# Columns of six weight units stored in another order and read back in the natural one by TensorE's access pattern

## The chip, the cores and the metric

The kernel runs on one core of one Trainium2 chip, in one launch. The metric is the device time of that launch in microseconds; the number given for a kernel is the median of its runs. The profile is one more execution, taken by the hardware profiler, with its own time.

The engines are named as in the profile: PE is TensorE (matmuls), PEld its weight loads, DVE is VectorE, ACT is ScalarE, POOL is GpSimd, SP issues most DMAs. A matmul has a stationary operand, which is loaded ahead as weights, and a moving operand, which is streamed through; its result is added up in PSUM.

## The reference: what is computed

One layer of a bidirectional encoder for 256 tokens of width 2,048. Twelve windowed attention heads and four Fourier groups make 2,048 features per token; they are normalised in two parts and go through the output projection, which the change touches. Then comes a feed-forward block with a convolution.

```python
        a = _rmsnorm(_window_attention(q, k, v, sink), attn_out_g)
        f = _rmsnorm(_fourier_mix(u, w_fourier), fourier_out_g)
        x = x + jnp.concatenate([a, f], axis=-1) @ w_out
        x = x + _conv_ffn(_rmsnorm(x, norm2_g), w_up, dw_w, dw_b, w_down)
    return _rmsnorm(x, normf_g)
```

`w_out` is 2,048 x 2,048 in float32.

## The kernel before

All large products are made in split float32: each operand is written as a high part (rounded to the type fp32r, which PE streams) and a low part, and three matmuls, high by high, low by high and high by low, are added in PSUM.

The weights come in *units* of 128 partitions x 2,048 values (1 MB). `load` (L166) issues a unit's DMA on SP into one of three `raw` buffers; `split` makes the high part with a Copy on ScalarE (L174) and the low part with a subtraction on VectorE (L175), both into a `parts` buffer (again three). `unit(i, work)` runs the matmuls of unit i and then splits unit i + 2 and loads further ones, so that splitting is two units ahead of PE and loading more. The order of the work on each engine is that of the program text; the small steps of attention and of the norms are hung before, beside or behind certain units (`at`, `run`).

The output projection has 16 units (`OUT_ORDER`, in the loop at L807). A unit is a pair (c, kq): the 512 output columns of block c, and the four k tiles (128 rows of `w_out` each) of group kq. The host lays them out with `moving` in `_layout`: for k tile q of the unit, `wout[n, :, 512 * q : 512 * (q + 1)]` holds its 128 rows in the partitions and its 512 columns side by side. In the output projection the weights are thus the *moving* operand, and the stationary one is a 128 x 128 piece of the activations, `cat` (the high part, then the low part of a tile, made by `feature_out`).

`moving_weights` (L339) makes the matmuls of a unit for one block of 128 tokens, b: for each k tile q, L345 streams the high weights against the high activations, L346 the high weights against the low activations, and L347 the low weights against the high activations. With two blocks and four k tiles that makes 24 matmuls of 512 columns in a unit, and 384 in the projection. Their results go to the PSUM tiles `ps_a` (groups 0 to 2, the attention features) and `ps_ff` (group 3, the Fourier features). The moving operand is one run of 512 adjacent values in each partition:

```python
            wh, wl = hi[:, q * n : (q + 1) * n], lo[:, q * n : (q + 1) * n]
```

When a group is complete, `out_add` (L766) adds the scaled sums to the residual `xs` on VectorE; when both groups of a block c are in, its columns are transposed on PE (`turn_x_in`, L789) for the next stage. The other callers of `moving_weights` are the projection of the values (`ps_v`, L602) and a part of the down projection (`ps_l`, L1199).

## Time and profile before

| | us |
|---|---|
| median of 3 runs | 946.41 (946.23 to 946.63) |
| the profiled execution | 945.75 |
| its span, first to last instruction | 944.0 |
| the first and last start of the output projection's matmuls | 162.1 and 256.5 |

The page of the profile gives the busy time of each engine, the chain of waits that ended last, and groups of equal instructions with busy time, mean duration, and the idle time of the engine just before them with what ended it. The timeline gives instructions in the order of time (start, duration, engine, line, operation, tiles, shape). A matmul's duration reaches from the start of its stream to its last result, and overlaps with the next matmul; the distance between two starts is what a matmul takes from PE. The granted clock of TensorE was 0.998 in the mean over the span.

### The profile page before, as it was taken

To read this page: it belongs to the slowest core of one execution; us is meant where nothing else is said; L and a number is where in the kernel's file an instruction comes from. 1 tells how busy PE (TensorE), PEld (TensorE's weight loads), DVE (VectorE), ACT (ScalarE), POOL (GpSimd) and SP (SyncE) were. 2 spreads that over 40 slices of the span, in tenths; PEclk is the share of its full clock that TensorE was granted. 3 is DMA by queue.
4 is the path that set the end of the run, shared out by engine and by line. 5 is a ranking of instruction groups with operands and counts; after the bars stand their busy time and mean duration, and the time that the engine had idled before them with its cause. 6 is when DMAs were issued, how large, how long until landed. Compare 5 with 4: busy or idle time off the path is not lost.

```text
span 944.0 us, 15017 instructions
## 1 busy us (share of the span) xinstructions
PE 934.7 (99%) x6275; PEld 857.6 (91%) x6275; DVE 711.1 (75%) x817; ACT 536.6 (57%) x624; POOL 48.2 (5%) x64
## 2 busy tenths in 40 slices
PE   9999999999999999999999999999999999999996
PEld 8889998888888999999999999999999999999985
DVE  7568877666667766869776887768878678889695
ACT  7656766554454645446555565555555555655544
POOL 0000000000000000000000000000000000000003
PEclk9999999999999999999999999999999999999999
DMA  9864544456558677677798778787787978779742
GB/s 361 312 224 137 176 140 173 134 179 202 195 223 271 220 232 238 188 241 238 250 261 257 243 238 274 249 264 228 261 242 238 298 249 256 248 217 265 222 176 89
DMA packets 32628, 215.00 MB, mean 228 GB/s; under 512 B 3600, under 2 KB 3856, under 8 KB 8240
## 3 DMA queue, kind: packets, MB, share of 16 engines
q1 hardware_dynamic: 28448, 184.55, 53.7%
q0 software_dynamic: 4112, 29.49, 16.5%
q8 instruction: 49, 0.80, 0.3%
q14 instruction: 19, 0.16, 0.0%
HBM read 211.93 MB, written 2.10 MB: 227 GB/s over the span
## 4 chain that ended last, share of the span: by engine, by line
PE 99%; POOL 0%; ACT 0%; issue 0%; DVE 0%; ACTq 0%; POOLq 0%
PE ps_val L375 22%; PE ps_gate L375 21%; PE ps_q L362 5%; PE ps_P L1081 3%; PE ps_P L1080 3%; PE ps_P L1079 3%; PE ps_N L1080 3%; PE ps_N L1081 3%; PE ps_N L1079 3%; PE ps_q L364 2%; PE ps_u L257 2%; PE ps_a L347 2%; PE ps_a L345 2%; PE ps_a L346 2%; PE ps_gate L362 2%; PE ps_val L362 2%
## 5 line engine op out<-in xcount | busy, mean ns | idle before, releaser
L175 DVE TENSOR_TENSOR parts<-raw,parts 128x2048 fp32r<-128x2048 f32 (+1 forms) x129 | 293.5, 2275 | 72.9 <-ACT parts L174 72.8
L174 ACT ACTIVATE parts<-raw 128x2048 fp32r<-128x2048 f32 (+1 forms) x129 | 245.9, 1906 | 82.2 <-PE ps_gate L375 19.9
L375 PEld LDWEIGHTS ps_val<-hU,parts 128*128 128x128 f32 x1824 | 211.6, 188 | 2.2
L375 PE MATMUL ps_val<-hU,parts 128*128 128x256 f32 x1824 | 212.9, 276 | 0.0
L375 PEld LDWEIGHTS ps_gate<-hU,parts 128*128 128x128 f32 x1776 | 206.4, 188 | 2.5
L375 PE MATMUL ps_gate<-hU,parts 128*128 128x256 f32 x1776 | 207.3, 276 | 0.0
L362 PE MATMUL ps_q<-hT,parts 128*128 128x512 f32 x192 | 66.0, 395 | 0.0
L856 ACT ACTIVATE fa_v<-ps_val 128x256 f32<-128x256 f32 x38 | 14.6, 384 | 88.3 <-PE ps_val L375 88.2
L966 DVE TENSOR_TENSOR parts_N<-sumw,parts_N 128x2048 fp32r<-128x2048 f32 x18 | 41.2, 2291 | 21.2 <-ACT parts_N L965 21.1
L1079 PE MATMUL ps_P<-parts_P,op_P 128*128 128x512 f32 x144 | 56.0, 389 | 0.0
L1080 PE MATMUL ps_P<-parts_P,op_P 128*128 128x512 f32 x144 | 56.0, 389 | 0.0
L1081 PE MATMUL ps_P<-parts_P,op_P 128*128 128x512 f32 x144 | 56.0, 389 | 0.0
L364 PE MATMUL ps_q<-hT,parts 128*128 128x256 f32 x192 | 51.6, 279 | 0.0
L362 PEld LDWEIGHTS ps_q<-hT,parts 128*128 128x128 f32 x192 | 35.9, 188 | 7.4
L965 ACT ACTIVATE parts_N<-sumw 128x2048 fp32r<-128x2048 f32 x18 | 34.4, 1914 | 14.3 <-PE ps_gate L375 10.6
L1079 PE MATMUL ps_N<-parts_N,op_N 128*128 128x512 f32 x108 | 42.0, 389 | 0.0
L1080 PE MATMUL ps_N<-parts_N,op_N 128*128 128x512 f32 x108 | 42.0, 389 | 0.0
L1081 PE MATMUL ps_N<-parts_N,op_N 128*128 128x512 f32 x108 | 42.0, 389 | 0.0
L345 PE MATMUL ps_a<-parts,cat 128*128 128x512 f32 x96 | 37.9, 395 | 0.0
L347 PE MATMUL ps_a<-parts,cat 128*128 128x512 f32 x96 | 37.5, 391 | 0.0
L346 PE MATMUL ps_a<-parts,cat 128*128 128x512 f32 x96 | 37.3, 389 | 0.0
L364 PEld LDWEIGHTS ps_q<-hT,parts 128*128 128x128 f32 x192 | 35.4, 188 | 0.3
(350 smaller groups left out, 1513.1 us busy)
## 6 DMA issues: line engine op xcount, KB each, us to landing
raw<-in_w_up SPq DMA_DIRECT2D x86, 1024.0 KB, 5.6
raw<-in_w_in SPq DMA_DIRECT2D x20, 1024.0 KB, 6.4
sumw<-in_w_down POOLq DMA_DIRECT2D x18, 1024.0 KB, 8.5
raw<-in_w_out SPq DMA_DIRECT2D x16, 1024.0 KB, 4.8
raw<-in_w_down_late SPq DMA_DIRECT2D x4, 1024.0 KB, 6.2
u_raw<-in_u_in SPq DMA_DIRECT2D x5, 768.0 KB, 10.8
raw<-in_w_down_last SPq DMA_DIRECT2D x4, 768.0 KB, 4.4
xs<-in_x SPq DMA_DIRECT2D x4, 512.0 KB, 15.3
```

Source lines behind the costliest of these rows:

```text
L174: nc.scalar.activation(hi, raw, AF.Copy)
L175: nc.vector.tensor_tensor(lo, raw, f32(hi), ALU.subtract)
L345: nc.tensor.matmul(ps, ah, wh, start=first and q == q0, stop=False)
L346: nc.tensor.matmul(ps, al, wh, start=False, stop=False)
L347: nc.tensor.matmul(ps, ah, wl, start=False, stop=last and q == q0 + len(kk) - 1)
L362: nc.tensor.matmul(ps, hi[:, s], h, start=k == 0, stop=False)
L364: nc.tensor.matmul(ps[:, 0:S], lo[:, s], h[:, 0:S], start=False, stop=k == NK - 1)
L375: nc.tensor.matmul(ps[:, 0:S], w[:, s], h[:, o : o + S], start=k == 0 and n == 0, stop=k == NK - 1 and n == 2,)
L966: nc.vector.tensor_tensor(lo, src, f32(hi), ALU.subtract)
L1079: nc.tensor.matmul(ps, o[:, 0, p, :], hi[:, s], start=first and p == 0, stop=False)
L1080: nc.tensor.matmul(ps, o[:, 1, p, :], hi[:, s], start=False, stop=False)
L1081: nc.tensor.matmul(ps, o[:, 0, p, :], lo[:, s], start=False, stop=end)
```

## The change

Six of the 16 units get a list of *forms*, one per k tile: units 1, 2, 4 and 6 one form for all four tiles, units 9 and 13 two forms each, for their second and fourth tile. A form (a, e, c) with a * e * c = 512 says that the host stores the 512 columns of that k tile in another order: column number ((e' * a) + a') * c + c' in the natural order stands at place ((a' * e) + e') * c + c'. `moving_weights` then describes the moving operand by three dimensions, e of step c, a of step e * c and c of step 1, so that PE reads the columns in the natural order again. The output columns in PSUM, the number and size of the DMAs, the splits and the number and order of the matmuls are as before.

In a partition, PE so reads c adjacent values, then c values that lie e * c values further, and so on for a pieces, and then begins again c values behind the first. With c = 1 there are no adjacent pairs: form (256, 2, 1) reads each second value, first the even places and then the odd ones; form (2, 256, 1) reads one value from the first half of the 512, one from the second half, and so on.

```diff
--- before.py
+++ after.py
@@ -53,6 +53,9 @@
 
 OUT_ORDER = [(0, 0), (1, 0), (0, 1), (1, 1), (0, 3), (0, 2), (1, 3), (1, 2)]
 OUT_ORDER += [(c, k) for c in (2, 3) for k in range(4)]
+
+OUT_FORMS = {1: [(2, 16, 16)] * 4, 2: [(2, 8, 32)] * 4, 4: [(4, 8, 16)] * 4, 6: [(2, 32, 8)] * 4}
+OUT_FORMS.update({9: [None, (2, 64, 4), None, (256, 2, 1)], 13: [None, (2, 256, 1), None, (8, 2, 32)]})
 
 
 GROUPS = [list(range(4))] + [list(range(k, k + 8)) for k in range(4, 36, 8)]
@@ -336,12 +339,17 @@
         nc.vector.tensor_copy(dst, spread_sums(spread_diagonals(r, name), name)[:, :S])
 
 
-    def moving_weights(hi, lo, n, kk, act, b, ps, first, last, q0=0):
+    def moving_weights(hi, lo, n, kk, act, b, ps, first, last, q0=0, forms=None):
 
         for q, k in enumerate(kk, q0):
             ah = act(k)[:, b * P : (b + 1) * P]
             al = act(k)[:, S + b * P : S + (b + 1) * P]
             wh, wl = hi[:, q * n : (q + 1) * n], lo[:, q * n : (q + 1) * n]
+            if forms and forms[q]:
+                a, e, c = forms[q]
+                wh, wl = (
+                    w.rearrange("p (a e c) -> p e a c", a=a, e=e, c=c) for w in (wh, wl)
+                )
             nc.tensor.matmul(ps, ah, wh, start=first and q == q0, stop=False)
             nc.tensor.matmul(ps, al, wh, start=False, stop=False)
             nc.tensor.matmul(
@@ -816,7 +824,7 @@
             for b in range(2):
                 moving_weights(
                     hi, lo, 512, range(4 * kq, 4 * kq + 4), cat.get, b, ps[b],
-                    kq in (0, 3), kq in (2, 3),
+                    kq in (0, 3), kq in (2, 3), forms=OUT_FORMS.get(n),
                 )
 
         unit(i, work)
@@ -1288,6 +1296,12 @@
     wout = np.concatenate(
         [moving(w_out, slice(c * 512, (c + 1) * 512))[k : k + 1] for c, k in OUT_ORDER]
     )
+    for n, forms in OUT_FORMS.items():
+        for q, form in enumerate(forms):
+            if form:
+                a, e, c = form
+                cols = wout[n, :, 512 * q : 512 * (q + 1)]
+                cols[:] = cols.reshape(P, e, a, c).transpose(0, 2, 1, 3).reshape(P, 512).copy()
     w_up = np.asarray(inp["w_up"])
     wup = np.concatenate(
         [still(w_up, o + j * P) for j in range(NF) for o in (0, DFF)]
```

## The prediction

> **What bounds the kernel now.** I read four views. First the page: busy time by engine, and the chain of waits that ended last.

> ```profile
> span 944.0 us, 15017 instructions
> PE 934.7 (99%) x6275; PEld 857.6 (91%) x6275; DVE 711.1 (75%) x817; ACT 536.6 (57%) x624; POOL 48.2 (5%) x64
> ...
> PE 99%; POOL 0%; ACT 0%; issue 0%; DVE 0%; ACTq 0%; POOLq 0%
> ```

> TensorE (PE) is busy for 99% of the span, and 99% of the chain is PE itself; issue and the other engines have 0%. A microsecond added to PE is therefore a microsecond added to the time, unless PE waits somewhere for something that comes no later. Next the costliest groups of the page, to see whether it waits in the stage that is changed:

> ```profile
> L175 DVE TENSOR_TENSOR parts<-raw,parts 128x2048 fp32r<-128x2048 f32 (+1 forms) x129 | 293.5, 2275 | 72.9 <-ACT parts L174 72.8
> L174 ACT ACTIVATE parts<-raw 128x2048 fp32r<-128x2048 f32 (+1 forms) x129 | 245.9, 1906 | 82.2 <-PE ps_gate L375 19.9
> ...
> L375 PE MATMUL ps_gate<-hU,parts 128*128 128x256 f32 x1776 | 207.3, 276 | 0.0
> ...
> L345 PE MATMUL ps_a<-parts,cat 128*128 128x512 f32 x96 | 37.9, 395 | 0.0
> L347 PE MATMUL ps_a<-parts,cat 128*128 128x512 f32 x96 | 37.5, 391 | 0.0
> L346 PE MATMUL ps_a<-parts,cat 128*128 128x512 f32 x96 | 37.3, 389 | 0.0
> ```

> The last column is idle time before the instruction: 0.0 for the three matmul lines of the output projection. The splitting Copies of ScalarE (L174) do have idle time, and what ends it is PE. So in this kernel PE sets the pace and the feeders wait.

> The mean of 389 ns is the latency of one matmul, which overlaps the next one; it is not what a matmul costs. That is the distance from start to start, so the third view is the timeline of PE, here one whole unit (12 matmuls for each of two row blocks) and, far behind it, a row of 256-column matmuls:

> ```profile
> 193.64 0.39 PE L345 MATMUL ps_a<-parts,cat 128*128 128x512 f32 x1
> 193.87 0.39 PE L346 MATMUL ps_a<-parts,cat 128*128 128x512 f32 x1
> 194.09 0.39 PE L347 MATMUL ps_a<-parts,cat 128*128 128x512 f32 x1
> ...
> 199.09 0.50 PE L485 MATMUL ps_tota<-ones,sq_a 128*128 128x1 f32 x4
> ```

> ```profile
> 500.27 3.00 PE L375 MATMUL ps_gate<-hU,parts 128*128 128x256 f32 x25
> ```

> From 193.64 to 199.09 there are 24 matmuls: 5.45 us / 24 = 227 ns each. The 25 matmuls of 256 columns take 3.00 us, of which the last one's latency is 0.276 us (L375 above): 2.72 / 24 = 113.5 ns. Twice the columns cost twice the time, so nothing fixed per matmul is left in the sum: PE takes one column of the moving operand each 227 / 512 = 0.443 ns. I call this a slot. PE reads the moving operand back to back and has no slack in which a slower read could hide.

> **The change part by part.** Nothing is added or removed on any queue: the same matmuls, splits and DMAs stand in the same order, and the DMAs carry the same bytes.

> *The permuted weights in HBM, their DMAs and the splits.* The permutation is made on the host, a row of a unit is still 2,048 contiguous values, and L174 and L175 go over it without looking at the order. Cost: 0. If a load were late, PE would show it; it has no idle time here.

> ```profile
> raw<-in_w_out SPq DMA_DIRECT2D x16, 1024.0 KB, 4.8
> ```

> *The longer description in the instruction.* The moving operand has three free dimensions in place of one. If PE's sequencer needs more time for it, this lies behind the matmul that streams: the row of 256-column matmuls shows that a weight load and a matmul are issued in 113.5 ns at the most, so 227 - 113 = 114 ns per matmul are cover. Cost: 0. Without the cover, it would be up to that much times 120 matmuls, which no row suggests.

> *The reads themselves.* This is the only term. A unit has 24 matmuls: four k tiles, two row blocks, three matmuls for each, and all three read the k tile's columns as moving operand. Units 1, 2, 4 and 6 permute all four k tiles (96 matmuls), units 9 and 13 two of four (12 each). That makes 120 matmuls, sorted by what a read looks like in a partition:
> - runs of 32, 16 or 8 adjacent values (units 1, 2, 4, 6 and the tile with form (8, 2, 32)): 102 matmuls;
> - runs of 4 adjacent values (form (2, 64, 4)): 6 matmuls;
> - no run at all, each value 8 bytes behind the last (form (256, 2, 1)): 6 matmuls;
> - no run, and each value 1,024 bytes from the last, to and fro (form (2, 256, 1)): 6 matmuls.

> No matmul of the trace reads its moving operand with steps, so the price is bounded from both sides. From below: 0, if any address is as good as the next. A gain is left out: 256-column and 512-column rows, in different stages and from different tiles, all run at the same 0.443 ns, and no row streams faster. From above, the rows where PE takes longest over a column:

> ```profile
> 0.99 4.37 PE L213 MATMUL ps_warm<-ones 128*128 128x128 f32 x20 [0.99 <-POOL ones L205]
> ...
> 205.03 1.04 PE L789 MATMUL ps_x<-ident,xs 128*128 128x128 f32 x8
> ...
> L789 PE MATMUL ps_x<-ident,xs 128*128 128x128 f32 x24 | 3.1, 273 | 0.0
> ```

> The transposes of the same stage: (1.04 - 0.27) / 7 = 110 ns for 128 columns, 0.86 ns a column, or two slots. The warm-up: ten matmuls (two records each) in 4.37 us, 3.4 ns a column, or 7.7 slots. Neither is a stepped read; they show at what rates PE can be held.

> My value: a run of 4 or more costs nothing, and a single value costs a second slot, as a column of the transposes does. The reason is the row above: the read streams 4 bytes per slot with no fixed part, so it must take neighbours together to keep up, and where the neighbour is not wanted, half of what is taken is thrown away. That gives 12 matmuls x 512 columns x 0.443 ns = 2.7 us. Bounds of this term: 0, and at the warm-up's 3.4 ns a column 12 x 512 x 2.97 = 18 us.

> *Where the added time goes.* The units lie in this stretch of PE's timeline (first and last start of a line's matmuls):

> ```profile
> L345 PE MATMUL ps_a<-parts,cat x96: 388/389/478, 162.1 to 250.6; 128*128 128x512 f32 x96
> L345 PE MATMUL ps_ff<-parts,cat x32: 389/389/476, 188.2 to 256.1; 128*128 128x512 f32 x32
> ```

> A later end of unit 9 or 13 delays the next unit's matmuls by as much; the splits for it (1.9 us on ScalarE, 2.3 us on VectorE by L174 and L175, against 5.45 us of PE per unit) only come earlier relative to PE. Nothing takes the time back later, since PE has no wait to shorten.

> Sum: the profiled execution took 945.75 us (span 944.0, and 1.75 around it); with 2.7 it would take 948.5. It lies 0.66 us under the median of 946.41 of the three runs, and the forecast is for the median: 946.41 + 2.72 = **949.1 us**.

> **The rivals.** A difference of 0.2%, 1.9 us, is about what a measurement of this kernel can tell from no change.

> *Only the to-and-fro form is slow, so the time does not move by more than that.* If what is fetched together is wide enough to hold two values that are 8 bytes apart, the form (256, 2, 1) finds two values per fetch and keeps its rate; only (2, 256, 1) changes place with each value. Place: the first of unit 13's two permuted k tiles. Price: 6 x 227 ns = 1.36 us, 947.8 us. It decides from the point at which an 8-byte step is free. For it: every other row of the trace is consistent with any width of fetch. Against it: the stream already runs at one value per slot, and nothing shows room for twice the bytes.
> [...]

> *Every break in a run costs.* If PE reads ahead along adjacent addresses and loses slots whenever the next value is elsewhere, all six units pay. Runs per matmul: 32, 16, 32 and 64 in units 1, 2, 4, 6 (24 matmuls each: 3,456), 128 for runs of 4, 512 to and fro, 16 for runs of 32 (6 matmuls each: 3,936); 7,392 breaks without the 8-byte form. At one slot: 3.3 us, 949.7. At the warm-up's extra 2.97 ns: 22 us, 968. I take two slots, near the transposes, since they run in this very stage: 6.6 us, 953.0. For it: a row after a change of work starts unevenly (the matmul at 199.45 is followed by the next only at 199.77), so PE does have a start-up in its reads. Against it: the matmuls of a row each start at a new address and pay nothing for that.

> ```profile
> 199.45 0.48 PE L345 MATMUL ps_ff<-parts,cat 128*128 128x512 f32 x1
> 199.77 0.39 PE L346 MATMUL ps_ff<-parts,cat 128*128 128x512 f32 x1
> ```

> *Any pattern with more than one free dimension leaves the fast read.* All 120 matmuls at half rate: 120 x 227 ns = 27 us, 973.7. Nothing in the trace speaks for it but that every moving operand there has one dimension.

> *Not slower at all.* Each value is addressed by itself and any order costs one slot: 946.4. It decides if even a 1,024-byte step costs nothing. For it: VectorE reads a row backwards in the time that it needs forwards.

> ```profile
> L563 DVE TENSOR_TENSOR y<-yh x4: 284/284/284, 65.4 to 85.5; 128x127 f32<-128x127 f32 x4
> L564 DVE TENSOR_TENSOR y<-yh x4: 283/284/286, 65.6 to 85.7; 128x127 f32<-128x127 f32 x4
> ```

> Against it: that is another engine, at a fifth of PE's rate (284 ns for 127 values, 2.2 ns each), and its values are still neighbours.

> **How the numbers follow.** Both single-value forms slow: 0.30. Breaks cost: 0.28. To and fro alone: 0.22. No cost: 0.14. All at half rate: 0.06. Slower by over 0.2%: 0.30 + 0.28 + 0.06 = 0.64. Within 0.2%: 0.22, and 0.12 of no cost: 0.34. Faster: 0.02, for what the reordered addresses might do that no row shows. The range goes from 946.4 (half of the no-cost case lies below) to 957.0, which is 3.2 slots per break; left out are 0.07 below, 0.06 for half rate and about 0.05 of the dearer breaks.

> **What would show it.** Start-to-start distances on PE in the six units, beside 227 ns in the untouched units. I expect 227 in units 1, 2, 4 and 6, and some 450 for six matmuls in unit 9 (its last k tile) and six in unit 13 (its second). If unit 9 is even, the to-and-fro rival holds; if unit 6 (runs of 8) is longer than unit 2 (runs of 32), breaks cost. The forecast is wrong from the ground if the distance is unchanged everywhere and the time still moves, or if units that were not touched change.

## The result and the profile after

| | before | changed |
|---|---|---|
| median of 12 runs each | 946.53 us (945.66 to 947.11) | 948.98 us (948.01 to 949.40) |
| ratio | | 1.0025, 95% interval 1.0017 to 1.0034 |
| span of the profiled execution | 944.0 us | 946.2 us |

The changed kernel is 2.45 us slower. The forecast was 949.1, from +2.72. The sum is right; the trace shows that its parts are not.

The page of the changed kernel: span, busy time by engine, the chain of waits, and the three groups of the output projection (their lines have moved by 8).

```profile
span 946.2 us, 15017 instructions
...
PE 936.9 (99%) x6275; PEld 857.8 (91%) x6275; DVE 711.3 (75%) x817; ACT 537.0 (57%) x624; POOL 48.2 (5%) x64
...
PE 99%; POOL 0%; ACT 0%; issue 0%; DVE 0%; ACTq 0%; POOLq 0%
...
L353 PE MATMUL ps_a<-parts,cat 128*128 128x512 f32 x96 | 38.6, 403 | 0.0
L355 PE MATMUL ps_a<-parts,cat 128*128 128x512 f32 x96 | 38.2, 398 | 0.0
L354 PE MATMUL ps_a<-parts,cat 128*128 128x512 f32 x96 | 38.1, 397 | 0.0
```

PE has 2.2 us more to do, the span is 2.2 us longer, nothing on PE waits anew (idle 0.0 before all three groups). The means of the groups hide what happened, since only some matmuls changed. The timeline of PE in unit 9, first row block (natural, runs of 4, natural, each second value; three matmuls each):

```profile
219.05 0.41 PE L353 MATMUL ps_a<-parts,cat 128*128 128x512 f32 x1
...
219.81 0.40 PE L353 MATMUL ps_a<-parts,cat 128*128 128x512 f32 x1
...
220.52 0.61 PE L353 MATMUL ps_a<-parts,cat 128*128 128x512 f32 x1
220.96 0.63 PE L354 MATMUL ps_a<-parts,cat 128*128 128x512 f32 x1
221.41 0.63 PE L355 MATMUL ps_a<-parts,cat 128*128 128x512 f32 x1
221.86 0.42 PE L353 MATMUL ps_a<-parts,cat 128*128 128x512 f32 x1
```

From start to start: 0.76 / 3 = 253 ns with runs of 4, and 1.34 / 3 = 447 ns with each second value (451 once settled). In unit 13 the second k tile reads to and fro:

```profile
243.33 0.38 PE L353 MATMUL ps_a<-parts,cat 128*128 128x512 f32 x1
243.54 0.38 PE L354 MATMUL ps_a<-parts,cat 128*128 128x512 f32 x1
243.76 0.38 PE L355 MATMUL ps_a<-parts,cat 128*128 128x512 f32 x1
243.97 0.39 PE L353 MATMUL ps_a<-parts,cat 128*128 128x512 f32 x1
```

By the starts in whole nanoseconds, 647 / 3 = 216 ns: one of the two orders that I took for the slowest is *faster* than the natural one with its 227. Unit 1 (runs of 16) is longer throughout: 24 matmuls from its first start to the next work, 5.76 us against 5.45 before, 240 ns each. First its two ends in the changed kernel, then in the kernel before:

```profile
168.41 0.40 PE L353 MATMUL ps_a<-parts,cat 128*128 128x512 f32 x1
...
174.17 0.40 PE L717 MATMUL ps_o<-pt,v_hi 128*128 128x256 f32 x2
```

```profile
168.74 0.39 PE L345 MATMUL ps_a<-parts,cat 128*128 128x512 f32 x1
...
174.19 0.40 PE L709 MATMUL ps_o<-pt,v_hi 128*128 128x256 f32 x2
```

By the starts of both traces, each unit against itself, in us:

| unit | order | change | forecast |
|---|---|---|---|
| 1 | runs of 16, two streams | +0.31 | 0 |
| 2 | runs of 32, two streams | +0.20 | 0 |
| 4 | runs of 16, four streams | +0.08 | 0 |
| 6 | runs of 8, two streams | +0.35 | 0 |
| 9 | runs of 4 | +0.15 | 0 |
| 9 | each second value | +1.32 | +1.36 |
| 13 | to and fro | -0.08 | +1.36 |
| 13 | runs of 32, eight streams | +0.05 | 0 |
| all | uneven starts of rows, here and in the units behind | +0.19 | 0 |
| sum | | +2.57 | +2.72 |

The span grew by less, 2.2, because the projection began 0.33 us earlier in this execution.

### The profile page after: what moved, and what is told of

Its sections match the earlier page's. It is cut to its first block, busy times and chain, and to the rows that moved or that the text cites. A ratio compares the mean times of both kernels' runs of the same rounds, so it can differ in the third digit from the quotient of the medians.

```text
span 946.2 us, 15017 instructions
## 1 busy us (share of the span) xinstructions
PE 936.9 (99%) x6275; PEld 857.8 (91%) x6275; DVE 711.3 (75%) x817; ACT 537.0 (57%) x624; POOL 48.2 (5%) x64
## 4 chain that ended last, share of the span: by engine, by line
PE 99%; POOL 0%; ACT 0%; issue 0%; DVE 0%; ACTq 0%; POOLq 0%
PE ps_val L383 22%; PE ps_gate L383 21%; PE ps_q L370 5%; PE ps_P L1087 3%; PE ps_P L1088 3%; PE ps_P L1089 3%; PE ps_N L1087 3%; PE ps_N L1089 3%; PE ps_N L1088 3%; PE ps_a L353 2%; PE ps_a L355 2%; PE ps_a L354 2%; PE ps_q L372 2%; PE ps_u L260 2%; PE ps_gate L370 2%; PE ps_val L370 2%
## 5 line engine op out<-in xcount | busy, mean ns | idle before, releaser
L178 DVE TENSOR_TENSOR parts<-raw,parts 128x2048 fp32r<-128x2048 f32 (+1 forms) x129 | 293.5, 2276 | 76.1 <-ACT parts L177 76.0
L177 ACT ACTIVATE parts<-raw 128x2048 fp32r<-128x2048 f32 (+1 forms) x129 | 245.9, 1906 | 86.0 <-PE ps_gate L383 19.9
L383 PE MATMUL ps_val<-hU,parts 128*128 128x256 f32 x1824 | 212.9, 276 | 0.0
L383 PE MATMUL ps_gate<-hU,parts 128*128 128x256 f32 x1776 | 207.3, 276 | 0.0
L353 PE MATMUL ps_a<-parts,cat 128*128 128x512 f32 x96 | 38.6, 403 | 0.0
L355 PE MATMUL ps_a<-parts,cat 128*128 128x512 f32 x96 | 38.2, 398 | 0.0
L354 PE MATMUL ps_a<-parts,cat 128*128 128x512 f32 x96 | 38.1, 397 | 0.0
## 6 DMA issues: line engine op xcount, KB each, us to landing
raw<-in_w_up SPq DMA_DIRECT2D x86, 1024.0 KB, 5.5
raw<-in_w_in SPq DMA_DIRECT2D x20, 1024.0 KB, 5.6
sumw<-in_w_down POOLq DMA_DIRECT2D x18, 1024.0 KB, 8.5
raw<-in_w_out SPq DMA_DIRECT2D x16, 1024.0 KB, 4.8
raw<-in_w_down_late SPq DMA_DIRECT2D x4, 1024.0 KB, 6.3
```

The source lines that it names most:

```text
L177: nc.scalar.activation(hi, raw, AF.Copy)
L178: nc.vector.tensor_tensor(lo, raw, f32(hi), ALU.subtract)
L353: nc.tensor.matmul(ps, ah, wh, start=first and q == q0, stop=False)
L354: nc.tensor.matmul(ps, al, wh, start=False, stop=False)
L355: nc.tensor.matmul(ps, ah, wl, start=False, stop=last and q == q0 + len(kk) - 1)
L383: nc.tensor.matmul(ps[:, 0:S], w[:, s], h[:, o : o + S], start=k == 0 and n == 0, stop=k == NK - 1 and n == 2,)
```

## The experiments

Times are medians; the kernel before ran on the same chip each time, and its median there is given.

### One of the two parts at a time

The runs alone, against the changed kernel:

```diff
-OUT_FORMS.update({9: [None, (2, 64, 4), None, (256, 2, 1)], 13: [None, (2, 256, 1), None, (8, 2, 32)]})
```

> Units 1, 2, 4 and 6 as in the change, units 9 and 13 in the natural order. By the starts in the trace of the changed kernel these four units took 0.31 + 0.20 + 0.08 + 0.35 = 0.95 us more than before: about 947.5 against 946.5 before (+0.10%). My forecast had 0 for them (946.5); the rival of breaks had most of its 6.6 us here.

Measured: 947.33 against 946.24, ratio 1.0012 (1.0003 to 1.0021), +1.1 us. The four units show +0.31, +0.20, +0.08 and +0.35 in the trace, as in the changed kernel; the projection as a whole is 0.93 us longer.

Each second value alone, against the kernel before:

```diff
+OUT_FORMS = {9: [None, None, None, (1, 256, 2, 1)]}
```

(From here on a form has a leading number, of blocks in each of which the pattern is run through; here it is 1.)

> Only the last k tile of unit 9 in form (256, 2, 1), six matmuls with 8-byte steps, everything else natural. By the trace of the changed kernel 6 x 220 ns = 1.3 us more than before, about 947.8 (+0.14%); my forecast had 1.36 for this form. If most of the 1.5 us of unit 9 came from its runs of 4, 0.3 us or less.

Measured: 947.94 against 946.24, ratio 1.0017 (1.0008 to 1.0025), +1.7 us; unit 9 is 1.37 us longer in the trace and no other unit moves by more than 0.04. The projection as a whole is 1.41 us longer. So by the starts the change is made, in the main, of two parts of 0.93 and 1.41 us, the first of which the forecast did not have. (The medians give 1.1 and 1.7 us, each uncertain by some 0.8.)

### Thirty orders side by side

Each of 15 units reads two neighbouring k tiles in one order and two in another:

```diff
-                a, e, c = forms[q]
-                wh, wl = (
-                    w.rearrange("p (a e c) -> p e a c", a=a, e=e, c=c) for w in (wh, wl)
-                )
+                m, a, e, c = forms[q]
+                how = "p (m a e c) -> p m e a c"
+                wh, wl = (w.rearrange(how, m=m, a=a, e=e, c=c) for w in (wh, wl))
...
+    (2, (1, 4, 128, 1), (1, 128, 4, 1)),
```

> Thirty orders, each for two neighbouring k tiles of a unit (12 matmuls); unit 0 keeps the natural order. In the trace of the changed kernel a 512-column matmul took 227 ns in the natural order, about 450 with each second value (8-byte step) and 216 to and fro between two halves 1,024 bytes apart. Theory of words: the fetch brings 8 bytes, PE keeps the last few, and a matmul is slow where a word gives only one value while it is kept; then step 4 (form 1,128,4,1) and step 8 (1,64,8,1) also cost about 450, all to-and-fro forms of few streams 216 to 227 whatever their distance, and pairs at any distance about 227. Theory of lines: the fetch brings 16 bytes or more at one line in four slots; then step 4 costs about 907, step 8 as much or twice that. Theory of distances (banks): what counts is the distance from one read to the next; then the to-and-fro forms with 8, 16, 32, 64, 128, 256, 512 bytes differ among each other, and the one with 8 bytes (128,2,2,1) is slow like step 2. Theory of breaks: cost goes by runs per matmul; then to and fro, with 512, could not be the fastest.

Measured: 970.31 us, in one execution. What it was for is the time from start to start of the settled matmuls (natural order: 227):

| order | ns per matmul |
|---|---|
| to and fro, distance 16, 32, 64, 128, 256, 512 or 1,024 bytes | 216 |
| to and fro, distance 8 bytes (0, 2, 1, 3, ...) | 226 to 236 |
| single values, 4 streams | 283 |
| single values, 8 streams; 16 streams | 487; 433 |
| step of 8, 16, 32, 64 bytes | 451, 460, 431, 434 |
| pairs, to and fro over 1,024 bytes; 4 streams | 340; 443 |
| pairs, step of 16 bytes (0, 1, 4, 5, ...) | 453 |
| runs of 4: two streams; four; eight | 246 to 260; 262 to 274; 266 to 287 |
| runs of 4, step of 32 bytes | 233 |
| runs of 8: two streams; four | 242; 231 |
| runs of 16: two streams; four | 240; 234 |
| runs of 32 | 233 to 241 |
| runs of 64, of 128 | 227 to 236 |

The timeline of unit 2, second row block, has the two kinds next to each other: three matmuls of four streams of single values, then three of 16-byte steps.

```profile
183.11 0.45 PE L369 MATMUL ps_a<-parts,cat 128*128 128x512 f32 x1
183.40 0.45 PE L370 MATMUL ps_a<-parts,cat 128*128 128x512 f32 x1
183.68 0.45 PE L371 MATMUL ps_a<-parts,cat 128*128 128x512 f32 x1
183.96 0.62 PE L369 MATMUL ps_a<-parts,cat 128*128 128x512 f32 x1
184.41 0.64 PE L370 MATMUL ps_a<-parts,cat 128*128 128x512 f32 x1
184.87 0.64 PE L371 MATMUL ps_a<-parts,cat 128*128 128x512 f32 x1
185.33 0.64 PE L369 MATMUL ps_a<-parts,cat 128*128 128x512 f32 x1
```

All four theories written down for this run fall. Words: pairs at 16-byte steps use whole words and cost 453. Lines, one in four slots: a 16-byte step should have cost 907 and costs 460, hardly more than 8 bytes. Distances: from 16 bytes on they make no difference to and fro. Breaks: the orders with 512 breaks per matmul, single values to and fro from 16 bytes on, are the fastest of the thirty (216).

### The two lanes put to the test

Orders in which the lanes and the other theories part, in units 9, 11, 13 and 15:

```diff
+S2 = "p (a e h) -> p h e a"
+OUT_FORMS = {
+    9: [(S2, dict(a=2, e=128, h=2))] * 2 + [(S2, dict(a=2, e=64, h=4))] * 2,
...
```

> Theory of two lanes, formed on the thirty orders: the first, third, fifth value of a stream go one way and the second, fourth, sixth another, and each way takes a 16-byte line in four slots and keeps it until it needs another. Natural order: each way needs every line, two values of it, just at the limit (227 ns). To and fro: each way stays in its own half and uses four values of a line (216). Each second value: each way uses one value of a line (453). The orders here are new. Unit 9, first two k tiles, and unit 11: to and fro over 1,024 bytes with 8-byte steps (0, 256, 2, 258, ...): by the two lanes each way uses two values of a line, 227 ns, although each 8-byte word gives one value; by the theory of words 453. Unit 9, last two: the same with 16-byte steps (0, 256, 4, ...): one value of a line, 453 by both. Unit 13, first two: four streams of 8-byte steps: at least the 283 of four streams, 453 if lines are not kept. Unit 13, last two: the control, 216. Unit 15: to and fro with 32-byte steps, 430 to 453, and 16 streams of 8-byte steps, 430 to 453.

Measured: 955.73 us, in one execution. Unit 9, second row block (two k tiles with 8-byte steps to and fro, then 16-byte steps):

```profile
222.53 0.42 PE L356 MATMUL ps_a<-parts,cat 128*128 128x512 f32 x1
222.78 0.39 PE L357 MATMUL ps_a<-parts,cat 128*128 128x512 f32 x1
223.01 0.39 PE L358 MATMUL ps_a<-parts,cat 128*128 128x512 f32 x1
223.24 0.39 PE L356 MATMUL ps_a<-parts,cat 128*128 128x512 f32 x1
...
223.92 0.61 PE L356 MATMUL ps_a<-parts,cat 128*128 128x512 f32 x1
```

8-byte steps to and fro: 227 ns, also in all 24 matmuls of unit 11, although no two values that follow each other are neighbours. 16-byte steps to and fro: 451. Both numbers had been written down, and for the first one the theory of words had 453. Steps of 32 bytes to and fro took 461, a little over the 430 to 453 that was expected, and 16 streams 440; four streams of 8-byte steps took 327 to 334, neither 283 nor 453. If there are lanes, a lane would have to keep more than one line for a while, and how many stays open. The lanes themselves are inferred from these times; no view shows them.

### How far the gain of the to-and-fro order carries

The whole output projection:

```diff
+OUT_FORMS = {n: [(1, 2, 256, 1)] * 4 for n in range(16)}
```

> All 64 k tiles of the output projection in form (2, 256, 1), to and fro over 1,024 bytes. If the 216 ns of six matmuls in the changed kernel belong to the form, all 384 matmuls take 216 in place of 227: 384 x 11 ns = 4.2 us less than before, about 942.3 us. If they were an accident of the place in unit 13 (phase against the weight loads), the gain is between 0 and 1 us. If several such tiles in a row fall back to the double time that I forecast for this form, 384 x 227 ns = 87 us more.

Measured: 942.29 against 946.24, ratio 0.9957 (0.9942 to 0.9972). The tile view of the 288 matmuls that write `ps_a` shows an even latency of 379 ns in place of 389, and the starts are 216 ns apart.

```profile
L351 PE MATMUL ps_a<-parts,cat x96: 377/379/463, 163.6 to 248.1; 128*128 128x512 f32 x96
L352 PE MATMUL ps_a<-parts,cat x96: 378/379/379, 163.8 to 248.3; 128*128 128x512 f32 x96
```

Then all weights that PE streams, in groups of eight columns (distance 16 bytes):

```diff
+def turns(w):
+    return w.rearrange("p (m a e) -> p m e a", a=2, e=4)
```

> Every weight that is a moving operand (first projections, output projection, down projection) is stored by the host so that each 8 columns stand as 0, 2, 4, 6, 1, 3, 5, 7, and read to and fro with 16 bytes between (216 ns in the thirty orders). If the gain belongs to the order wherever PE sets the pace: 96 + 96 + 384 + 756 + 96 + 63 = 1,491 matmuls of 512 columns x 11 ns = 16.4 us less than before, about 930. If VectorE (75% busy) becomes the bound in the down projection, where 756 of them are, the gain stays at 8 to 10 us, about 937.

Measured: 950.47 against 946.06, ratio 1.0048 (1.0030 to 1.0066): slower, and outside both expectations. The 1,491 matmuls did settle at 216 ns, and VectorE held nothing up: none of PE's idle time is put down to it. The time went into instructions that were not touched, the 256-column matmuls of the up projection. Their groups here, one of them in the kernel before, and a stretch of 42 starts here (4.99 / 42 = 119 ns):

```profile
L380 PE MATMUL ps_val<-hU,parts 128*128 128x256 f32 x1824 | 222.9, 280 | 0.0
L380 PE MATMUL ps_gate<-hU,parts 128*128 128x256 f32 x1776 | 217.1, 280 | 0.0
```

```profile
L375 PE MATMUL ps_val<-hU,parts 128*128 128x256 f32 x1824 | 212.9, 276 | 0.0
```

```profile
499.74 5.15 PE L380 MATMUL ps_gate<-hU,parts 128*128 128x256 f32 x42
504.73 0.38 PE L1084 MATMUL ps_N<-parts_N,op_N 128*128 128x512 f32 x1
```

222.9 + 217.1 against 212.9 + 207.3 before: the busy time shows 19.8 us more, 118.9 ns from start to start in place of 113.3, with no wait. To find out whether that comes from the to-and-fro rows next to them, the 756 products of the down projection were left natural:

```diff
-            nc.tensor.matmul(ps, o[:, 0, p, :], turns(hi[:, s]), start=first and p == 0, stop=False)
+            nc.tensor.matmul(ps, o[:, 0, p, :], hi[:, s], start=first and p == 0, stop=False)
```

> As the run with all weights, but the 756 matmuls of the products of the down projection (L1079 to L1081 of the kernel before), which stand among the up projection's natural 256-column rows, stay natural. In the run with all weights those 3,600 untouched matmuls went from 113.3 to 118.9 ns each (20 us). If that comes from entering a natural row behind a to-and-fro row, which only the products do there, they are back at 113.3 and the time is 735 x 11 ns = 8.1 us less than before, about 938. If it comes from anything earlier in the kernel, they stay at 118.9 and the time is about 12 us more than before, 958.

Measured: 938.44 against 946.36, ratio 0.9919 (0.9903 to 0.9936), as expected, with the same groups back at their old values:

```profile
L380 PE MATMUL ps_val<-hU,parts 128*128 128x256 f32 x1824 | 212.9, 276 | 0.0
L380 PE MATMUL ps_gate<-hU,parts 128*128 128x256 f32 x1776 | 207.3, 276 | 0.0
```

So these natural rows of 256 columns run at 118.9 when the products between them are read to and fro, and the gain of 756 matmuls is more than given back by 3,600 others. It is no rule for every natural row behind a to-and-fro row: in the run with all weights, the first part of the up projection follows the to-and-fro output projection and settles within four pairs at 227 and 113 ns (it alternates 512 and 256 columns). Why the rows of 256 columns alone do not settle stays open; nothing in them waits, and their own instructions are the same.

The remedy is to take these rows to and fro as well. The up projection's activations are written so that even and odd tokens stand apart:

```diff
+            hi, lo = (t.rearrange("p (a e) -> p e a", a=2) for t in (hi, lo))
+            src = src.rearrange("p (e a) -> p e a", a=2)
...
-                nc.tensor.matmul(ps, hi[:, s], h, start=k == 0, stop=False)
+                nc.tensor.matmul(ps, hi[:, s], read(h), start=k == 0, stop=False)
```

> As the run with all weights, and the up projection's activations hU too: VectorE and ScalarE write the even tokens of a k tile into the first half and the odd ones into the second (512 bytes apart), PE reads to and fro. It has 3,776 matmuls of 256 columns at 113.3 ns and 176 of 512. If half of a 512-column matmul's gain holds for 256 columns (109 ns): 3,776 x 4.2 + 176 x 11 = 17.8 us more gain, about 912. If the weight load sets the pace there (a 128 x 128 load lasts 188 ns and one starts each 113), 1.9 us more, about 928. If the longer writes of hU at the start of the up projection hold PE up, up to 32 x 0.5 = 16 us back.

Measured: 922.14 against 946.06, ratio 0.9748 (0.9733 to 0.9764).

```profile
L387 PE MATMUL ps_val<-hU,parts 128*128 128x256 f32 x1824 | 209.8, 275 | 0.0
L387 PE MATMUL ps_gate<-hU,parts 128*128 128x256 f32 x1776 | 204.5, 275 | 0.0
```

The time lies between the two that were expected, 912 and 928. The matmuls take 111.7 ns each, between the 109 of the first and the 113.3 of the second, a limit by the weight load. The first part of the up projection has 109 for its 256 columns, and 219 for its 512. Does the place of the weights in their buffer make the difference? Against the run before:

```diff
+    SPOTS = [(0, 32), (0, 0), (0, 16), (16, 16), (28, 28), (0, 8), (0, 4), (8, 40), (0, 48), (0, 64)]
...
+        if place == "thirds":
+            SPOTS.append(SPOTS.pop(0))
+            PLACES[place] = SPOTS[-1]
```

> As the run with the up projection; the weights of the later up projection start at ten different places in their buffer, unit by unit (0 to 64 values further on). There a 256-column matmul took 111.7 ns against 109.1 in the earlier part of the up projection, whose low weights start 16 values further on in place of 32. If the weight load's place against the moving read makes the 2.6 ns, the units differ by it and the ones with 16 are at 109; if it is the order of high and low parts, all ten stand at 111.7.

Measured: 921.97 us in one execution; all ten places stand at 111.7 ns, and the two groups have 209.8 and 204.5 us as above. The place is not the reason. Last, the queries and keys, against the run with the up projection:

```diff
-        nc.vector.tensor_tensor(add, ps[:, 0:S], tmp, ALU.add)
+        there = add.rearrange("p (a e) -> p e a", a=2)
+        one, two = (t.rearrange("p (e a) -> p e a", a=2) for t in (ps[:, 0:S], tmp))
+        nc.vector.tensor_tensor(there, one, two, ALU.add)
...
-            still_weights(hi, lo, ps, range(NK), OPENING.get((kind, h), 0), lambda h: h)
+            still_weights(hi, lo, ps, range(NK), lag=OPENING.get((kind, h), 0))
```

> As the run with the up projection, and the queries' and keys' products too read hT to and fro between the two halves of 256 tokens; their columns come out in that order and VectorE puts them back when it adds the two partial sums. 256 matmuls of 512 columns at 231 (L362 ps_q 232, ps_k 228) and 256 of 256 at 116: 256 x (14 + 6) = 5 us less than the run with the up projection, about 917. If VectorE's stepped writes are twice as long, its share in that stage grows by 16 x 0.4 us and nothing changes on PE; if the weight load sets the pace of these matmuls, no gain, 922.

Measured: 919.61 against 946.36, ratio 0.9719 (0.9704 to 0.9733): 2.5 us less than the run with the up projection (2.8 when each is compared with the kernel before on its own chip), not 5. The matmuls gained what was expected (ps_q from 233 to 220 and from 117 to 110; 4.8 us by the starts, with the keys), but PE now waits at a line where it never waited before:

```profile
L723 PE MATMUL ps_o<-pt,v_hi 128*128 128x256 f32 x48 | 9.7, 289 | 1.4 <-DVE pt L714 1.4
```

1.4 us are this wait for VectorE's split of the attention weights. By the starts the `ps_o` matmuls take 2.0 us longer in all, and two smaller groups, `ps_t` and `ps_u`, 0.3 each, which leaves 2.2 of the 4.8. That VectorE is late because its sums `add_q` now take 609 ns each in place of 419 is likely, but no run takes them apart. This kernel beats the one before by 27 us and the changed one by 29.

## Why the prediction was right in its sum and wrong in its parts

*PE sets the end.* Right. Every change of the distance between two starts appears in the time; PE had no wait in this stage before and has none after. That held for the gains too, but for 0.7 us of waits for ScalarE in the run with the whole projection, 0.4 us for VectorE in the run with the up projection and 1.9 us in the last one.

*Host order, DMAs, splits and the longer description cost nothing.* Right: in the run with each second value alone, nothing but unit 9 and the start of unit 10 moves (no unit but 9 by more than 0.04 us). In the changed kernel the loads of `w_out` land in 4.8 us as before, and the splits of all 129 units are busy for 245.9 us on ScalarE and 293.5 on VectorE as before. A pattern with more dimensions is no cost in itself, since 216 ns were reached with three of them.

*Each second value costs a second slot.* Right in size: 6 x 227 = 1.36 forecast, 1.32 measured. The reason given, that the neighbour in the fetched word is thrown away, is not the one: 8-byte steps to and fro would throw away as much and run at 227.

*A single value to and fro costs a second slot too.* This is the step that failed: "a single value costs a second slot, as a column of the transposes does", applied to form (2, 256, 1). It measured 216 ns against 227, 0.08 us less instead of 1.36 more, and so it did for all 384 matmuls of the projection. The forecast reasoned from neighbours in the stream; what fits most single values, in the thirty orders and the test after them, is how many values of a 16-byte line each of two alternating lanes uses. That this is the mechanism is argued, not shown. And "a gain is left out" fell with it: that natural rows run at 0.443 ns a column (most of them do; the matmuls of ps_q took 232 and 116 ns) showed a limit of the natural order, not of PE.

*Runs of 4 or more cost nothing.* Wrong: units 1, 2, 4 and 6 alone cost 1.1 us by the medians, 0.94 by their starts. The rival of breaks had this, at two slots for each break, and its sign came in: unit 6 grew by more than unit 2 (0.35 against 0.20). Unit 1 measures 13 ns for 32 breaks, about one slot each, unit 6 some 15 ns for 64, half a slot, and to and fro with 512 breaks is below zero. So breaks cost, but not by their number. Nor does the number of streams order them: with runs of 16 two streams cost more than four (240 against 234 ns), with runs of 4 less (246 to 260 against 262 to 274). What makes it stays open; the two lanes as told here don't explain it.

The missing cost of the runs (about 1.1 us) and the cost that the to-and-fro form did not have (1.36, and the 0.08 gained) nearly cancel; 0.19 of uneven starts makes up part of the rest. The time was met by two errors of opposite sign, not by the mechanism.

*Only the to-and-fro form is slow*, the first rival. Wrong in both its parts: each second value, which it had at the natural rate, took 451 ns, and to and fro over 1,024 bytes, which it had at twice the time, took 216 against 227. In the thirty orders to and fro is fast at every distance from 16 to 1,024 bytes (216 ns) and not at 8 (226 to 236).

## What to carry to other kernels

Where PE sets the pace and streams 4-byte values, look at the distance from start to start per column, not at the latency, and do not take the natural order for the best: to and fro between two places 16 to 1,024 bytes apart went from 227 to 216 ns for 512 columns, and the host can store weights so: the loads and splits of the changed kernel took no longer than before (4.8 us to land; 245.9 and 293.5 us of splitting in all). Look at the rows next to them, since what is gained may be given back there: 1,491 faster matmuls made the kernel 4 us slower through 3,600 others, and it became faster both when the 756 that stand among those stayed natural (by 8 us) and when the 3,600 were read to and fro too (by 24 us). And check a forecast by its parts in the trace: a sum that comes out right proves none of its terms.

## What the runs showed of the hardware that was not expected

A matmul of 512 columns takes 227 ns in natural order and 216 to and fro (219 where it alternates with 256 columns); 256 columns take 113.3 and 109 to 111.7. Steps of 8 bytes double the time if the stream takes them one after the other (451), and cost nothing against the natural order if it alternates between two such streams (227). Identical instructions of 256 columns took 113.3 ns or 118.9, depending on the order in which the rows between them were read.
